# Recording the second layer's attention mixer and ordering it as one list-scheduled stage

## The chip, the cores and the metric

The kernel runs on one core of a Trainium2 chip. The metric is the device time of one execution in microseconds (us); the median of the runs is compared. PE is the matrix engine TensorE, PEld its weight loads, DVE is VectorE, ACT is ScalarE, POOL is GpSimd, SP is SyncE, which here mostly issues DMAs.

## The reference

The reference is a two-layer trunk on 16 learned tokens followed by 1024 inputs (1040 positions), width 1024. Layer 0 has an RWKV and pooling mixer, layer 1 a differential attention mixer; each is followed by an MLP. The attention, which is what matters here:

```python
def causal_diff_attention(q, k, v, lam):
    ...
        s = jnp.einsum('bqhcd,bkhcd->bhcqk', qblk, k).astype(jnp.float32) * scale
        qpos = start + jnp.arange(Q_BLOCK)
        mask = kpos[None, :] <= qpos[:, None]
        s = jnp.where(mask, s, -jnp.inf)
        p = jax.nn.softmax(s, axis=-1)
        attn = p[:, :, 0] - lam * p[:, :, 1]
        return jnp.einsum('bhqk,bkhe->bqhe', attn.astype(v.dtype), v)
    ...

def diff_attn_mixer(h, w_in, lam_vecs, subln_w, w_out, cos, sin, layer):
    ...
    q = apply_rope(q.reshape(B, L, DIFF_HEADS, 2, DIFF_HEAD), cos, sin)
    k = apply_rope(k.reshape(B, L, DIFF_HEADS, 2, DIFF_HEAD), cos, sin)
    ...
    o = causal_diff_attention(q, k, v, lam)
    o = rmsnorm(o, subln_w, SUBLN_EPS) * (1.0 - lam_init)
    return o.reshape(B, L, D_MODEL).astype(h.dtype) @ w_out
```

There are 8 heads; each has two halves c = 0, 1 of q and k, each half with a softmax of its own.

## The kernel before

Every fp32 product is made of three products of high and low parts, so matmuls come in triples (lines 377, 378 and 379 for the projections, 1895 to 1897 for the mix). `mixer1` is the attention mixer. `attn_in(h)` makes the input of head h: for k, q and v in turn, three chunks of 346 or so positions, each a group of 24 matmuls into one bank of the pool `dps` (two banks; `psq`, `psv`), then on DVE the rotary products `rp`, `ab` (`rows`), for k and q the DMAs that regroup the two halves into `qkd` (`heads`, eight issues on SP's queue for each of k and q), the casts to a high part on ACT and a low part on DVE (`halves`: `kh`, `kl`, `qst`); for v the product with `rsa` (`vt`), transposes `pst` and the casts `vh`, `vl` (`turn`). `rsa` holds 1/rms of each position; `settle` (line 485) sums squares over partitions with one matmul for a chunk of positions and makes it. The projections themselves read the unnormalized `opa` and do not need `rsa`; what follows them does.

`attn(h)` makes four groups g = 0 to 3 of two blocks of 128 queries. For each block `attn_block` makes scores `s` (two halves in the pool `sps`, two tiles), maximum, exp on ACT (line 1842), the sums and the difference `p` on DVE. `flip` transposes `p` to a single bank `tr` (`tps`), which ACT casts to `ah` and DVE to `al`; `tail` does it for the 16 last positions (`trx`, line 1879, one for each group); `mix` multiplies by v into the single bank `av`; `square` and `norm` finish a half of the head. `soft` in head h makes the blocks of the next group, or the first two blocks of head h+1. While `attn(h)` runs, the steps of `attn_in(h+1)` are written between its steps at the places of the table `at`; in the last head, steps of the output projection (`early`, tiles `pse`) are written there.

In `mixer1` all this is issued directly, and the framework decides each engine's order. The stage of layer 0 is made otherwise: a `Recorder` takes each instruction with a price for its engine and the regions it reads and writes; `Flow.order` then sorts them by a list schedule (the engine that can start earliest takes the ready task with the longest rest of chain) and `Flow.run` writes them out under `manual_schedule`, where this order holds. Ring buffers (`Ring`) fix which buffer each tile has. A task with no recorded writer before it counts as ready from the start.

Of the kernel before, what the change touches and what calls it, by code (L numbers as in the profile page):

```python
# [8 lines left out]
F32R = mybir.dt.float32r  # L9
# [190 lines left out]
class Recorder:  # L200
# [8 lines left out]
    @contextlib.contextmanager  # L209
    def group(self):  # L210

        self.held = []
        yield
        calls, self.held = self.held, None
        if calls:
            self.keep(calls[0][0], sum(c[1] for c in calls), [c[2] for c in calls], [x for c in calls for x in c[3]], [x for c in calls for x in c[4]], False, 0)
# [43 lines left out]
    def call(self, eng, op, args, kw):  # L260
# [12 lines left out]
        elif eng == "PE":  # L273
            cols, x = math.prod(int(k) for k in args[0].shape[1:]), args[1]
            if x.dtype == F32R:
# [46 lines left out]
class Trunk:  # L322
# [22 lines left out]
    def group(self):  # L345
        return self.nc.group() if isinstance(self.nc, Recorder) else contextlib.nullcontext()
# [1289 lines left out]
    def mixer1(self, hn):  # L1636
# [4 lines left out]
        with tc.tile_pool(name="dps", bufs=2, space=PSUM, reuse_waits="tile") as dps, \  # L1641
# [3 lines left out]
             tc.tile_pool(name="ep", bufs=1, reuse_waits="tile") as ep:  # L1645
            self.dps, self.sps, self.tps, self.aps, self.ep = dps, sps, tps, aps, ep
# [34 lines left out]
            for h in range(8):  # L1681
                nxt, side = self.attn_in(h + 1, hn) if h < 7 else (None, fill[:30])
                main = self.attn(h, qkv, nxt)
                at = (0, 6, 12, 12, 14, 15, 16, 24, 24, 24, 24, 24, 24, 24, 29, 29) if h < 7 else [0 + i * 2 for i in range(len(side))]
# [13 lines left out]
            self.late_x = xs  # L1698
        return part
# [101 lines left out]
    def attn_block(self, h, i, qkv):  # L1801
# [7 lines left out]
        for c in (0, 1):  # L1809
# [7 lines left out]
            for a in range(0, L, 512):  # L1817
# [8 lines left out]
                if x1 > x0:  # L1826
                    nc.tensor.matmul(out(x0, x1), self.identb, self.maskb[:, x0 - m0:x1 - m0], start=False, stop=True)
# [30 lines left out]
    def attn(self, h, qkv, nxt):  # L1858
# [27 lines left out]
        def mix(g, j0):  # L1886
# [5 lines left out]
            if j0 < 2 * g + 2:  # L1892
                for j in (j0, j0 + 1):
                    sl = slice((j - j0) * 256, (j - j0) * 256 + 256)
                    nc.tensor.matmul(o, vh[:, j], ah[:, sl], start=(j == 0), stop=False)  # L1895
                    nc.tensor.matmul(o, vl[:, j], ah[:, sl], start=False, stop=False)
                    nc.tensor.matmul(o, vh[:, j], al[:, sl], start=False, stop=False)
            else:
                o1, j = o[:, P:], j0
                nc.tensor.matmul(o1, vh[:NM, j], ah[:NM], start=False, stop=False)  # L1900
                nc.tensor.matmul(o1, vl[:NM, j], ah[:NM], start=False, stop=False)
                nc.tensor.matmul(o1, vh[:NM, j], al[:NM], start=False, stop=True)
# [35 lines left out]
        for g in range(4):  # L1938
# [145 lines left out]
```

## Time and profile before

| | |
|---|---|
| median of 3 runs | 2788.69 us (2782.02 to 2795.86) |
| the profiled execution's own time | 2794.32 us |
| span of its profile | 2792.5 us |
| mean granted clock of TensorE | 0.969 of full |
| PE busy | 2626.3 us, 94% of the span |
| DVE, ACT, POOL busy | 2043.4, 1345.2, 292.5 us |

The span is from the first instruction to the last. The attention mixer's part begins around 1406 us with its first projections and ends at 2039 us, where the output projection's last matmul of the stage starts. A busy PE is not PE at its peak, since matmuls overlap and their ends are modelled.

### The profile page before, as it was taken

The page shows a single profiled execution, that of the slowest core. Times are in us where ns is not written, and L with a number is a line of the kernel's source. Part 1 is how long each engine was busy: PE and PEld are TensorE (multiplying, and loading weights), DVE is VectorE, ACT ScalarE, POOL GpSimd, SP SyncE. Part 2 cuts the span into 40 slices and gives each one's busy share as a digit, 9 for nine tenths or more (in the row PEclk, how much of TensorE's full clock was granted, in tenths as well). Part 3 has the DMA queues.
Part 4 walks back from the last instruction along what each step waited for, and adds up shares of the span by engine and source line. Part 5 has one row for each costly group of instructions (what it writes and reads, how often), then busy time and mean ns, then how long its engine had stood idle before and what let it go on. Part 6 is the DMA issues. An engine that isn't in the chain of part 4 may idle for free.

```text
span 2792.5 us, 44856 instructions
## 1 busy us (share of the span) xinstructions
PE 2626.3 (94%) x16950; PEld 2389.0 (86%) x16950; DVE 2043.4 (73%) x3742; ACT 1345.2 (48%) x2779; POOL 292.5 (10%) x410
## 2 busy tenths in 40 slices
PE   7999997899999999999968999999889999999997
PEld 6899897799899999999957899898786788778877
DVE  5356866634977778888785887888648778778888
ACT  6456766544533335333334556556645333443342
POOL 0111334230000000000012222222000000000000
PEclk9999999899999999999978999999999999999998
DMA  4456767554423345443332222222243243553443
GB/s 154 168 191 193 233 207 220 175 148 156 146 107 148 146 172 191 168 153 135 99 113 69 61 74 71 61 67 63 81 153 130 106 166 131 197 185 136 151 159 121
DMA packets 198576, 391.28 MB, mean 140 GB/s; under 512 B 59984, under 2 KB 122328, under 8 KB 185944
## 3 DMA queue, kind: packets, MB, share of 16 engines
q1 hardware_dynamic: 171176, 348.24, 37.6%
q10 hardware_dynamic: 27184, 40.18, 4.0%
q8 instruction: 133, 2.18, 0.3%
q14 instruction: 83, 0.68, 0.1%
HBM read 240.06 MB, written 131.38 MB: 133 GB/s over the span
## 4 chain that ended last, share of the span: by engine, by line
PE 66%; DVE 9%; ACT 3%; issue 2%; DMA 2%; POOL 0%; SPq 0%; DVEq 0%; ACTq 0%; POOLq 0%
PE bank L690 46%; PE psq L377 2%; PE psq L378 2%; PE psq L379 2%; PE ps L292 1%; PE s L1823 1%; PE s L1825 1%; PE tr L1869 1%; PE xs L292 1%; ACT p L1842 1%; PE bank L732 1%; PE av L1895 1%; DVE ac L767 1%; DVE p L1855 1%; DVE ac L1072 1%
## 5 line engine op out<-in xcount | busy, mean ns | idle before, releaser
L690 PE MATMUL bank<-opa,wp 128*128 128x260 f32 (+1 forms) x3296 | 656.3, 319 | 5.8 <-DVE wp L781 3.5
L690 PEld LDWEIGHTS bank<-opa,wp 128*128 128x128 f32 x3296 | 517.2, 189 | 55.6 <-DVE wp L781 5.0
L690 PE MATMUL bank<-opb,wp 128*128 128x260 f32 (+1 forms) x1150 | 347.6, 323 | 3.0 <-DVE ac L1000 3.0
L292 PE MATMUL ps<-opa,whi 128*128 128x346 f32 (+2 forms) x1008 | 270.3, 330 | 5.3 <-DVE ys L292 4.1
L690 PE MATMUL bank<-opa,hh 128*128 128x260 f32 (+1 forms) x1112 | 240.8, 321 | 7.5 <-DVE hh L781 5.3
L690 PEld LDWEIGHTS bank<-opb,wp 128*128 128x128 f32 x1150 | 216.2, 188 | 22.1 <-ACT opa L1023 3.4
L1000 DVE TENSOR_TENSOR ac<-bank,ac 128x520 f32<-128x520 f32 (+1 forms) x256 | 171.1, 691 | 67.1 <-PE bank L690 65.1
L690 PE MATMUL bank<-opa,opb 128*128 128x260 f32 (+4 forms) x1168 | 204.7, 305 | 11.4 <-DVE opb L670 5.4
L690 PEld LDWEIGHTS bank<-opa,hh 128*128 128x128 f32 x1112 | 185.7, 191 | 24.0 <-DVE hh L781 5.8
L292 PEld LDWEIGHTS ps<-opa,whi 128*128 128x128 f32 x1008 | 182.2, 194 | 7.5 <-DVE ys L292 4.9
L690 PEld LDWEIGHTS bank<-opa,opb 128*128 128x128 f32 x1168 | 167.6, 193 | 22.3 <-DVE opb L670 5.8
L690 PE MATMUL bank<-opb,hh 128*128 128x260 f32 (+1 forms) x616 | 180.4, 326 | 0.0
L780 ACT CAST wp<-raw 128x512 fp32r<-128x512 f32 (+1 forms) x138 | 80.4, 584 | 199.3 <-PE bank L690 191.7
L292 PE MATMUL ps<-opa,wlo 128*128 128x346 f32 (+2 forms) x504 | 158.8, 315 | 0.0
L780 ACT CAST wp<-ss 128x512 fp32r<-128x512 f32 (+1 forms) x130 | 76.4, 589 | 165.4 <-PE bank L690 141.0
L1842 ACT ACTIVATE p<-s,m 128x272 f32<-128x272 f32 (+7 forms) x128 | 95.6, 751 | 86.1 <-DVE m L1838 84.4
L690 PE MATMUL bank<-opa,tt 128*128 128x260 f32 (+1 forms) x648 | 131.1, 320 | 2.2 <-DVE ac L1000 2.0
L690 PEld LDWEIGHTS bank<-opb,hh 128*128 128x128 f32 x616 | 117.5, 191 | 10.0
L377 PE MATMUL psq<-opa,wp 128*128 128x346 f32 (+2 forms) x352 | 118.0, 335 | 4.4 <-DVE rp L462 2.6
L362 POOL TENSOR_TENSOR wpx<-raw,wp 128x1024 fp32r<-128x1024 f32 (+1 forms) x14 | 34.4, 2459 | 789.6 <-PE bank L690 745.3
L379 PE MATMUL psq<-opa,wp 128*128 128x346 f32 (+2 forms) x352 | 113.9, 324 | 0.0
L690 PE MATMUL bank<-opb,opb 128*128 128x256 f32 (+4 forms) x456 | 111.3, 307 | 1.4 <-DVE tt L746 1.4
(408 smaller groups left out, 6587.4 us busy)
## 6 DMA issues: line engine op xcount, KB each, us to landing
raw<-in_w_dram SPq DMA_DIRECT2D x64, 1024.0 KB
hid<-ac SPq DMA_DIRECT2D x14, 1820.0 KB
hid<-ac SPq DMA_DIRECT2D x14, 1792.0 KB
hh<-hid SPq DMA_DIRECT2D x23, 1040.0 KB
hh<-hid SPq DMA_DIRECT2D x23, 1024.0 KB
pk<-sg ACTq DMA_DIRECT2D x32, 704.0 KB
lt<-pk SPq DMA_DIRECT2D x32, 704.0 KB
raw<-in_w_qkv_dram SPq DMA_DIRECT2D x24, 512.0 KB
```

The lines of the kernel that those rows point to most:

```text
L292: one = eng, cost, lambda: fn(*args, **kw), r, w
L362: (lo or nc.gpsimd).tensor_tensor(lw[:, :n], raw[:, :n], hi[:, :n].bitcast(F32), op=ALU.subtract)
L377: nc.tensor.matmul(ps, wh, xh, start=(first and i == 0), stop=False)
L378: nc.tensor.matmul(ps, wl, xh, start=False, stop=False)
L379: nc.tensor.matmul(ps, wh, xl, start=False, stop=(last and i == n - 1))
L690: nc.tensor.matmul(ps, use(x), use(y), start=start and i == j == 0, stop=i == len(ws) - 1 and j == 2, skip_group_check=not start)
L732: nc.tensor.matmul(acc, ones, use(src), start=first, stop=last)
L767: F.dve(NH, lambda mk=mk, k=k: stt(mk, mk, self.gcol(l, 1, k), y, op0=ALU.mult, op1=ALU.mult), r=nm + [("T", 2)], w=nm)
L780: F.act(n, lambda: nc.scalar.copy(use(t[0][:, :n]), src), r=rd, w=[z[0]] + claim)
L1000: F.dve(NH, lambda d=d, q=q: tt(sv(d), q, sv(d), op=ALU.add), r=nq + nd, w=nd, ps=True)
L1072: F.dve(W, lambda d=d, k=k: tt(d, d, use(H3[k // 4][:, k % 4, :W]), op=ALU.add), r=nd + [("H", k // 4, k % 4)], w=nd)
L1842: nc.scalar.activation(p[:, :L0], S[c][:, :L0], AF.Exp, bias=m2[:, c:c + 1], scale=0.125, accum_out=m2[:, 2 + c:3 + c])
```

## The change

`mixer1` makes a `Recorder`, wraps its pools in rings of the same sizes, and runs the flow at its end. The three matmuls of a score or of a mix step are kept together as one recorded task (`group`; with `whole` the task counts as writing its whole bank, for the first of a group of mixes). A transpose is priced at 0.115 in the recorder. The places of the next head's steps (`at`) and their sequence are changed, and `pair` takes the mix of two steps ago ahead of the flip. The computation and the number of instructions on the matrix of each head stay.

```diff
@@ class Recorder
-    def group(self):
+    def group(self, whole=False):
...
-            self.keep(calls[0][0], sum(c[1] for c in calls), [c[2] for c in calls], [x for c in calls for x in c[3]], [x for c in calls for x in c[4]], False, 0)
+            w = [x for c in calls for x in c[4]]
+            self.keep(calls[0][0], sum(c[1] for c in calls), [c[2] for c in calls], [x for c in calls for x in c[3]], [x.tensor[:] for x in w[:1]] if whole else w, False, 0)
...
-            if x.dtype == F32R:
+            if op == "transpose":
+                cost = .115
+            elif x.dtype == F32R:
...
@@ mixer1
+            rec = Recorder(tc)
+            self.nc = nc = rec
+            dps, sps, tps, aps = [Ring(x, n, least) for x, n, least in ((dps, 2, 512), (sps, 2, 1024), (tps, 1, 512), (aps, 1, 512))]
+            ep = Ring(ep, 1)
...
-                at = (0, 6, 12, 12, 14, 15, 16, 24, 24, 24, 24, 24, 24, 24, 29, 29) if h < 7 else [0 + i * 2 for i in range(len(side))]
+                if h < 7:
+                    side = [side[i] for i in (0, 1, 2, 3, 5, 6, 7, 10, 11, 4, 8, 9, 12, 13, 14, 15)]
+                at = (0, 6, 12, 12, 15, 16, 18, 20, 22, 25, 25, 25, 25, 25, 29, 29) if h < 7 else [0 + i * 2 for i in range(len(side))]
...
+            rec.flow.run()
+        self.nc = tc.nc
...
@@ attn_block
-                nc.tensor.matmul(out(a, b), st[:, qs], kh[:, a:b], start=True, stop=False)
                 x0, x1 = max(a, m0), min(b, L)
-                nc.tensor.matmul(out(a, b), st[:, qs], kl[:, a:b], start=False, stop=x1 <= x0)
...
+                with self.group():
+                    nc.tensor.matmul(out(a, b), st[:, qs], kh[:, a:b], start=True, stop=False)
+                    nc.tensor.matmul(out(a, b), st[:, qs], kl[:, a:b], start=False, stop=x1 <= x0)
...
@@ attn, mix
-                    nc.tensor.matmul(o, vh[:, j], ah[:, sl], start=(j == 0), stop=False)
...
+                    with self.group(j == 0):
+                        nc.tensor.matmul(o, vh[:, j], ah[:, sl], start=(j == 0), stop=False)
...
@@ attn, the order of flips and mixes
+                if i >= 2:
+                    pair.append(ms[i - 2])
                 if i < n:
                     pair.append(ts[i])
-                if i >= 2:
-                    pair.append(ms[i - 2])
```

In the changed program all instructions of the mixer have the recorder's line 295, and the tiles have the names of the rings: `ps_0` and `ps_1` are the two banks of `dps`, `s_0` and `s_1` those of `sps`, `vt_0` to `vt_2` a ring of three that `p` uses too, `spare` the ring of `vh` and `vl`. Outside the mixer the order of every engine is the same in both programs.

First place, PE where the stage begins. Before, 49 projection matmuls into `s` stand between the last matmul of the stage ahead (line 732) and the first `settle` (line 485); here are the last of them:

```order
L379 MATMUL s_13735<-opa_74,wp_6332 128x346
L377 MATMUL s_13735<-opa_75,wp_6332 128x346
L378 MATMUL s_13735<-opa_75,wp_6333 128x346
L379 MATMUL s_13735<-opa_75,wp_6332 128x346
L485 MATMUL ps_13848<-rsa,con 128x346
L378 MATMUL s_13737<-opa_70,wpx 128x332
L379 MATMUL s_13737<-opa_70,wp_6334 128x332
```

In the changed program the settle follows that last matmul at once:

```order
L735 MATMUL bank_6368<-ss_6356,con 128x346
L295 MATMUL ps_0_13735<-rsa,con 128x346
L295 MATMUL s_0_13728<-opa_70,wp_6332 128x348
L295 MATMUL s_0_13728<-opa_70,wp_6333 128x348
L295 MATMUL s_0_13728<-opa_70,wp_6332 128x348 x2
```

So the settle has moved ahead of those 49 projections.

Second place, DVE while head 0's input is finished: `kl` is the low part of k's halves, `rp` and `ab` here are the rotary products of head 1. Before:

```order
L1787 TENSOR_TENSOR vl_13875<-pst_14074,vh_13874 16x128
L1763 TENSOR_TENSOR kl_14009<-qkd_13998,kh_14008 128x640
L1731 TENSOR_TENSOR rp_14144<-psq_14119,cs 64x348
L1732 TENSOR_TENSOR rp_14144<-psq_14119,cs 64x348
L1731 TENSOR_TENSOR rp_14244<-psq_14219,cs 64x346
L1733 TENSOR_TENSOR ab_14118<-psq_14119,cs 128x348
L1732 TENSOR_TENSOR rp_14244<-psq_14219,cs 64x346
L1763 TENSOR_TENSOR kl_14014<-qkd_14003,kh_14013 128x640
```

Changed:

```order
L295 TENSOR_TENSOR vt_0_13741<-ps_0_13735,rsa 128x346
L295 TENSOR_TENSOR kl_0_13748<-qkd_0_13744,kh_0_13746 128x640
L295 TENSOR_TENSOR kl_1_13749<-qkd_1_13745,kh_1_13747 128x640
L295 TENSOR_TENSOR spare_1_13740<-ps_0_13735,spare_1_13738 128x512
L295 TENSOR_TENSOR spare_1_13740<-ps_1_13736,spare_1_13738 128x512
L295 TENSOR_TENSOR spare_1_13740<-ps_1_13736,spare_1_13738 16x128
L295 TENSOR_TENSOR rp_2_13734<-ps_0_13735,cs 64x348 x2
L295 TENSOR_TENSOR qst_0_13750<-qkd_0_13744,qst_0_13750 64x1024
```

Both halves of `kl` now stand together, ahead of head 1's rotary products; before, five of those stood between them.

Third place, PE in the last head, at the transposes of group 2 and the scores around them; `pse` before, and `ps_0` and `ps_1` after, are output projection work that fills. Before:

```order
L1827 MATMUL s_19690<-maskb,identb 128x128
L379 MATMUL pse_19543<-opa_73,wp_6332 128x256
L1869 MATMUL tr_19594<-con,p_19498 128x128
L1869 MATMUL tr_19594<-con,p_19473 128x128
L1869 MATMUL tr_19594<-con,p_19498 128x128
L1823 MATMUL s_19744<-kh_18790,qst_19023 128x512
L1825 MATMUL s_19744<-kl_18791,qst_19023 128x512
L1823 MATMUL s_19744<-kh_18790,qst_19023 128x512
L1895 MATMUL av_19707<-ah_19599,vh_19033 128x256
```

Changed:

```order
L295 MATMUL tr_0_13757<-con,vt_1_13742 128x128
L295 MATMUL tr_0_13757<-con,vt_2_13743 128x128
L295 MATMUL ps_0_13735<-opa_77,wp_6332 128x256
L295 MATMUL ps_0_13735<-opa_77,wp_6333 128x256
L295 MATMUL ps_0_13735<-opa_77,wp_6332 128x256
L295 MATMUL ps_1_13736<-opa_71,wp_6334 128x256
L295 MATMUL ps_1_13736<-opa_71,wpx 128x256
L295 MATMUL ps_1_13736<-opa_71,wp_6334 128x256
L295 MATMUL ps_0_13735<-opa_77,wp_6332 128x256
L295 MATMUL ps_0_13735<-opa_77,wp_6333 128x256
L295 MATMUL ps_0_13735<-opa_77,wp_6332 128x256
L295 MATMUL av_0_13764<-ah_2_13760,spare_0_13737 128x256
```

Where a transpose was followed by the next block's scores and the mix, three triples of filling work now stand between the transposes and the mix.

## Rows read from the trace of the kernel before

**Rows 1.** The page: busy time by engine, and the shares of the chain that ended last.

```profile
PE 2626.3 (94%) x16950; PEld 2389.0 (86%) x16950; DVE 2043.4 (73%) x3742; ACT 1345.2 (48%) x2779; POOL 292.5 (10%) x410
PE 66%; DVE 9%; ACT 3%; issue 2%; DMA 2%; POOL 0%; SPq 0%; DVEq 0%; ACTq 0%; POOLq 0%
```

**Rows 2.** Windows of the mixer: from:to and length in us, busy us (x instructions) of each engine, granted clock of PE, DMA share, GB/s.

```profile
1436.00:1490.00 54.00, 48.73 (x274) 46.45 (x275) 32.10 (x60) 13.28 (x23) 19.16 (x15) 0.92 0.24 60
1490.00:1555.00 65.00, 54.73 (x304) 45.57 (x303) 44.77 (x81) 34.08 (x69) 14.51 (x13) 0.87 0.26 71
1685.00:1750.00 65.00, 64.24 (x425) 58.41 (x424) 53.03 (x100) 38.02 (x76) 17.56 (x16) 1.00 0.24 66
1945.00:1985.00 40.00, 30.67 (x167) 23.39 (x166) 31.25 (x71) 27.52 (x68) 0.58 (x3) 0.90 0.21 67
1985.00:2025.00 40.00, 40.00 (x313) 38.10 (x312) 18.18 (x34) 21.54 (x50) 5.66 (x3) 0.97 0.25 81
```

**Rows 3.** Timeline of PE where the stage begins: start, duration, engine, line, out<-in, and in brackets the idle time before with what ended it.

```profile
1406.33 1.52 PE L732 MATMUL bank<-ss,con 128*128 128x346 f32 x2 [4.46 <-DVE ss L682]
...
1409.62 0.49 PE L377 MATMUL s<-opa,wp 128*128 128x348 f32 x1
1409.90 0.49 PE L378 MATMUL s<-opa,wp 128*128 128x348 f32 x1
...
1421.17 0.32 PE L379 MATMUL s<-opa,wp 128*128 128x346 f32 x1
1436.08 1.52 PE L485 MATMUL ps<-rsa,con 128*128 128x346 f32 x2 [14.60 <-DVE rsa L682]
```

**Rows 4.** Timeline of DVE while head 0's input is finished.

```profile
1474.46 0.83 DVE L1763 TENSOR_TENSOR kl<-qkd,kh 128x640 fp32r<-128x640 f32 x1 [0.61 <-ACT kh L1761]
...
1481.75 0.52 DVE L1731 TENSOR_TENSOR rp<-psq,cs 64x346 f32<-64x346 f32 x1 [2.86 <-PE psq L379]
...
1483.40 1.18 DVE L1763 TENSOR_TENSOR kl<-qkd,kh 128x640 fp32r<-128x640 f32 x1
...
1496.28 1.22 DVE L1756 TENSOR_TENSOR qst<-qkd,qst 64x1024 fp32r<-64x1024 f32 x1
```

**Rows 5.** Timeline of ACT there.

```profile
1480.43 1.05 ACT L1755 CAST qst<-qkd 128x1024 fp32r<-128x1024 f32 x1 [5.04 <-DMA qkd<-ab]
1489.74 1.05 ACT L1755 CAST qst<-qkd 128x1024 fp32r<-128x1024 f32 x1 [8.26 <-DMA qkd<-ab]
1499.39 0.38 ACT L1842 ACTIVATE p<-s,m 128x144 f32<-128x144 f32 x1 [8.60 <-DVE m L1838]
```

**Rows 6.** Timeline of PE: the transpose `trx` of group 3 in heads 0, 1, 2 and 6, and the last matmul of the stage.

```profile
1559.16 0.27 PE L1879 MATMUL trx<-con,p 128*16 128x128 f32 x1
...
1626.94 0.27 PE L1879 MATMUL trx<-con,p 128*16 128x128 f32 x1
...
1691.72 0.27 PE L1879 MATMUL trx<-con,p 128*16 128x128 f32 x1
...
1950.46 0.28 PE L1879 MATMUL trx<-con,p 128*16 128x128 f32 x1
...
2038.97 0.27 PE L379 MATMUL pse<-opa,wp 128*128 128x256 f32 x1
```

**Rows 7.** Timeline of PE: starts that follow each other without a wait, for projections of 346 columns (21 instructions lie between the two shown starts), a mix of 256, and scores of 512.

```profile
1467.09 0.33 PE L377 MATMUL psv<-opa,spare 128*128 128x346 f32 x1
...
1470.41 0.32 PE L377 MATMUL psv<-opa,spare 128*128 128x346 f32 x1
...
1745.00 0.28 PE L1896 MATMUL av<-ah,vl 128*128 128x256 f32 x1
1745.12 0.28 PE L1897 MATMUL av<-al,vh 128*128 128x256 f32 x1
...
1525.58 0.39 PE L1825 MATMUL s<-kl,qst 128*128 128x512 f32 x1
1525.81 0.34 PE L1823 MATMUL s<-kh,qst 128*128 128x400 f32 x1
```

**Rows 8.** PE in one steady head by tile, in this order: `psq`, `psv`, `av`, `tr`, `s`. Window, length, busy us (x instructions), clock, DMA share, GB/s.

```profile
1685.00:1750.00 65.00, 25.89 (x144) 1.00 0.24 66
1685.00:1750.00 65.00, 11.84 (x72) 1.00 0.24 66
1685.00:1750.00 65.00, 12.46 (x73) 1.00 0.24 66
1685.00:1750.00 65.00, 6.79 (x43) 1.00 0.24 66
1685.00:1750.00 65.00, 13.96 (x70) 1.00 0.24 66
```

**Rows 9.** Waits by engine, line and what was waited for: us in total, times, longest us. The first two in 1945 to 1990 us, the last in 1685 to 1750 us.

```profile
PE tr L1869 <- DVE p L1855: 4.0, 3, 2.2
PE s L1823 <- ACT p L1842: 2.8, 3, 1.8
...
DVE qst L1756 <- ACT qst L1755: 0.3, 1, 0.3
```

**Rows 10.** Timeline of SP's queue in head 0: the eight DMA issues of q's regrouping; the duration is from the first issue to the last one's end.

```profile
1607.46 5.26 SPq L1747 DMA_DIRECT2D qkd<-ab  x8
```

More of the change, by code (lines that the diff above doesn't have):

```diff
@@ L343, in nm, with group @@
         return f"{s}{self.uid}"
-    def group(self):
-        return self.nc.group() if isinstance(self.nc, Recorder) else contextlib.nullcontext()
+    def group(self, whole=False):
+        return self.nc.group(whole) if isinstance(self.nc, Recorder) else contextlib.nullcontext()
     def weights(self, src, n=1024, lo=None, pool=None):
@@ L1822, in attn_block @@
                     out = lambda x0, x1: se[:, c * NM + x0 - 1024:c * NM + x1 - 1024]
-                nc.tensor.matmul(out(a, b), st[:, qs], kh[:, a:b], start=True, stop=False)
                 x0, x1 = max(a, m0), min(b, L)
-                nc.tensor.matmul(out(a, b), st[:, qs], kl[:, a:b], start=False, stop=x1 <= x0)
-                if x1 > x0:
-                    nc.tensor.matmul(out(x0, x1), self.identb, self.maskb[:, x0 - m0:x1 - m0], start=False, stop=True)
+                with self.group():
+                    nc.tensor.matmul(out(a, b), st[:, qs], kh[:, a:b], start=True, stop=False)
+                    nc.tensor.matmul(out(a, b), st[:, qs], kl[:, a:b], start=False, stop=x1 <= x0)
+                    if x1 > x0:
+                        nc.tensor.matmul(out(x0, x1), self.identb, self.maskb[:, x0 - m0:x1 - m0], start=False, stop=True)
             S.append(sp)
@@ L1894, in mix @@
                     sl = slice((j - j0) * 256, (j - j0) * 256 + 256)
-                    nc.tensor.matmul(o, vh[:, j], ah[:, sl], start=(j == 0), stop=False)
-                    nc.tensor.matmul(o, vl[:, j], ah[:, sl], start=False, stop=False)
-                    nc.tensor.matmul(o, vh[:, j], al[:, sl], start=False, stop=False)
+                    with self.group(j == 0):
+                        nc.tensor.matmul(o, vh[:, j], ah[:, sl], start=(j == 0), stop=False)
+                        nc.tensor.matmul(o, vl[:, j], ah[:, sl], start=False, stop=False)
+                        nc.tensor.matmul(o, vh[:, j], al[:, sl], start=False, stop=False)
             else:
                 o1, j = o[:, P:], j0
-                nc.tensor.matmul(o1, vh[:NM, j], ah[:NM], start=False, stop=False)
-                nc.tensor.matmul(o1, vl[:NM, j], ah[:NM], start=False, stop=False)
-                nc.tensor.matmul(o1, vh[:NM, j], al[:NM], start=False, stop=True)
+                with self.group():
+                    nc.tensor.matmul(o1, vh[:NM, j], ah[:NM], start=False, stop=False)
+                    nc.tensor.matmul(o1, vl[:NM, j], ah[:NM], start=False, stop=False)
+                    nc.tensor.matmul(o1, vh[:NM, j], al[:NM], start=False, stop=True)
         sb = lambda: ep.tile([P, 512], F32, tag="sb", name=self.nm("sb"), bufs=4)
```

## The prediction

> **What bounds the kernel now.** I read the page first, then windows over the mixer, then single timelines. PE is busy 94% of the span and makes 66% of the chain that ended last, with DVE at 9% [rows 1]; the change touches nothing outside the mixer, so the rest of the program's time is taken as it is. Inside the mixer the windows show three different places [rows 2]. A steady head (1685 to 1750) has PE busy 64.24 of 65 us at full clock: nothing else is the limit there. The opening (1436 to 1555) has only 274 + 304 = 578 matmuls in 119 us where a steady head has 425 in 65: PE idles 5.27 + 10.27 = 15.5 us, and the clock, at 0.92 and 0.87, costs another 0.08 x 54 + 0.13 x 65 = 12.8 us. The tail (1945 to 1985) has PE busy 30.67 of 40 us, 9.3 idle, with a clock of 0.90, and the 40 us behind it 0.97: 4.0 + 1.2 = 5.2 us more. So what an order can give back is some 28 us in the opening, 14.5 in the tail, and little in a steady head.
>
> The stage splits at markers, the transpose of group 3's last 16 positions [rows 6]: the opening and head 0 end at 1559.16; six heads follow to 1950.46 (391.3 us; 67.8 for the first, 64.8 each for the others); the tail ends with the last matmul at 2038.97 (88.5 us).
>
> **The change part by part.** No instruction is added or removed, so each price is one of waits and of places. What a matmul costs PE without a wait is the distance of starts [rows 7]: 0.158 us for a projection ((1470.41 - 1467.09) / 21), 0.12 for a mix, 0.23 for 512 score columns.
>
> *Opening and head 0.* What it loses: before, the first 49 projections run from 1407.7 to 1421.2, at 0.28 us each, in time in which PE otherwise waits for the row sums; it then idles 14.60 us until the settle at 1436.08 [rows 3]. In the changed order the settle stands first, and PE takes its queue in order, so these 49 run after 1436: 49 x 0.158 = 7.7 us (13.7 if all went at half the clock). No other engine covers that.
>
> What it gives: before, DVE makes the first `kl` at 1474.46, then stands behind head 1's rotary products, which wait for projections (2.86 us at 1481.75), and reaches the second `kl` only at 1483.40 [rows 4]. q's second regrouping waits on it, ACT's casts of q wait 5.04 and 8.26 us for it, the low part of q ends on DVE at 1497.5, and the first exp starts at 1499.39 [rows 5]. By then PE has done five chunks of head 1's projections, which it lacks afterwards, when head 0's softmax leaves it idle. In the new order the two `kl` stand together. Following the new rows by hand with the durations of these views, I get 1456 for the settle of the third chunk, 1466 for k's DMAs, both `kl` at 1474 to 1476, the q DMAs from 1480, and the first exp near 1490, nine us earlier in spite of the 7.7.
>
> How much of it reaches the end: from the settle to the end of head 0 the new order has 687 matmuls: 462 projections at 0.158 = 73.0; 57 mixes at 0.12 = 6.8; 61 transposes and the like at 0.11 = 6.7; 22,080 score columns at 0.23 per 512 = 9.9; masks, tails, settles and norm, an estimate, 6. That is 102 us. Before, without the 49, it was 102 - 7.7 = 94.3, against 1559.16 - 1436.08 = 123.1 in the trace: 28.8 lost, which agrees with the 28.3 of the windows. After, I keep 11 of it: the half clock at the start, which no edit touches (some 4), and 7 of waits for the settles, the first DMAs and the single `tr` bank. So it ends at 1436.1 + 102 + 11 = 1549, **-10 us**. The bounds: if nothing is won but the 49 are late, +8; if only the clock's 3 are left, -18.
>
> *Six heads.* One head is 216 projections [rows 8] x 0.158 = 34.1; 60 mixes x 0.12 + 12 tails x 0.16 = 9.1; 56 transposes x 0.11 = 6.1; scores of 18,944 columns = 8.5 and 20 masks that hold up the next matmul by about 0.12 = 2.5; norm and the 16 column scores 2.2: 62.5 us, against 64.8. The Trainium skill ("Perfetto Trace Analysis", section "Identifying the Most-Contended Engine") says that matmul busy time misleads, since matmuls are pipelined, and that the busy share of the weight loads tells more. Here that share is 58.41 of 65 [rows 2], which by that rule would leave 6.6 us a head or 39 in six; the busy row alone would leave 0.76, or 4.6 in six; the trace's distances stand between them at 2.3.
>
> At most 2.3 x 6 + 3 (the first interval's excess) = 16 us are there. I take 0.5 for each of five heads and 2.5 of the 3, since the new places spread the input of head 1: **-5 us**. A fixed order that fits worse than the old one costs; I bound it by 1 us a head, the size of the idle that a steady head has now (0.76): +6.
>
> *Tail.* Before, transposes wait 4.0 us for `p` and scores 2.8 for ACT's exps [rows 9], while projection triples that could run stand behind them in PE's queue; in the new order such triples stand between transposes, scores and mixes. Of 9.3 idle and 5.2 clock I take 7 and 4: **-11 us**. The bounds: 0, if the waits only move, and -14, if all is filled. Behind the last norm as many filling matmuls are left as before, so the end has no new gap.
>
> *Edits at nothing.* The transposes' price, the groups of three, the table `at` and the sequence in `pair` only move places in the list, and are in the three terms. Groups cost nothing while PE has other work; without it a group waits for its latest input, within the bound of 1 us a head.
>
> **The sum.** -10 - 5 - 11 = -26. The profiled execution took 2794.3 (span 2792.5) and would take 2768 (span 2766.5); it lies 5.6 above the median of the runs, so the median goes from 2788.7 to **2763**. All bounds on one side: -48 (2741) and +14 (2803).
>
> **The rivals.** *Only the opening moves.* In a steady head PE is busy 64.24 of 65, and the tail's waits are those of a chain (scores, exp, `p`, transpose) that no order shortens. For it: DVE and ACT are busy 31.25 and 27.52 of the tail's 40 us [rows 2]. Against it: the filling triples need nothing of that chain. Time 2779 (-8 to -18).
>
> *Nothing comes back.* The 7.7 us of deferred projections are paid and the earlier exp only moves where PE waits next, at the softmax of head 0: 2789 to 2797.
>
> *Slower: q's DMAs come too late in every head.* The recorder prices an issue on SP at 0.47; the row has 5.26 / 8 = 0.66 for each of eight [rows 10], so k and q together are 3 us later than the list believes. DVE's order, now fixed, has `qst` ahead of the `al` of group 3's flips, so the single `tr` bank stays full, and PE with its transposes stands. At 3 us a head and seven heads it takes back 21 of the 26; it makes the kernel slower by more than 14 us from (26 + 14) / 7 = 5.7 a head. With the 8.26 that ACT waits at this place in the opening [rows 5] it is 26 - 58 = 32 slower: 2821. Against it: `qst` waits 0.3 us in a steady head now [rows 9], and in both orders it stands among the same `al`.
>
> **How the numbers follow.** About 14 us (0.5%) is what the runs, 2782 to 2796, can tell from no change. Chances: the forecast 0.60 (all faster); only the opening 0.15 (0.07 faster, 0.08 same); nothing back 0.13 (same); slower 0.12. So faster 0.67, same 0.21, slower 0.12. The range reaches from 2740, all gains, to 2803, all losses within the bounds; it leaves out the slower rival and a little below. The forecast's own range is 2745 to 2774.
>
> **What would show it.** The settle at 1436 with the 49 projections behind it; the first exp near 1490; the `tr` transpose of 16 positions of head 0's group 3 near 1549, of head 6 near 1935, the last matmul near 2013; a clock above 0.95 in the tail. I am wrong if the first exp stays near 1499, if the steady heads take over 65 us, or if `qst` waits for `qkd` over 2 us in a steady head.

## The result and the profile after

The changed kernel takes 2798.61 us (median of 12 runs, 2789.99 to 2806.78), the kernel before 2789.18 us in 12 runs beside it (2780.71 to 2797.76): ratio 1.0035, 95% interval 1.0023 to 1.0047. That is 9.4 us slower, a small loss within the 0.5% that the prediction called no change, but with so many runs its sign is clear; 2763 was forecast. The profiled execution took 2806.78 us (span 2805.0), 8 above its median, as that of before was 5 above its own. Of run e3 below, the profiled execution was a slow one (span 2878.2 us), so only the order of its rows is used.

Page of the changed kernel, busy time by engine and the chain that ended last:

```profile
PE 2617.9 (93%) x16950; PEld 2383.0 (85%) x16950; DVE 2034.1 (73%) x3742; ACT 1346.3 (48%) x2779; POOL 292.1 (10%) x410
PE 63%; DVE 10%; ACT 4%; DMA 2%; issue 2%; POOL 0%; SPq 0%; DVEq 0%; ACTq 0%; POOLq 0%
```

PE is less busy in a longer span, and DVE and ACT have taken 2 points of the chain from it [rows 1]: the instructions are as many as before, the waits are more. Windows of the changed kernel's mixer (columns as in [rows 2]):

```profile
1437.00:1490.00 53.00, 48.88 (x276) 47.02 (x277) 29.51 (x53) 14.79 (x24) 16.22 (x13) 0.91 0.26 71
1490.00:1555.00 65.00, 59.75 (x386) 52.14 (x384) 50.08 (x95) 35.41 (x75) 18.44 (x14) 1.00 0.24 66
1685.00:1750.00 65.00, 63.22 (x414) 57.02 (x413) 49.62 (x99) 37.84 (x76) 16.38 (x14) 1.00 0.23 65
1945.00:1985.00 40.00, 28.27 (x161) 22.87 (x160) 30.75 (x66) 26.41 (x63) 3.24 (x4) 0.79 0.25 68
```

Beside [rows 2], the second part of the opening has 82 matmuls more and the full clock; the steady head has 11 fewer in the same 65 us; the tail has 6 fewer, and its clock is 0.79 instead of 0.90. PE of the changed kernel, where the stage begins, and four of its group-3 tails (heads 0, 5, 6, 7; the transpose is now named `tr`, as ring buffers share names):

```profile
1407.91 1.52 PE L735 MATMUL bank<-ss,con 128*128 128x346 f32 x2 [4.47 <-DVE ss L685]
1437.75 1.49 PE L295 MATMUL ps<-rsa,con 128*128 128x346 f32 x2 [28.32 <-DVE rsa L685]
...
1559.10 0.27 PE L295 MATMUL tr<-con,vt 128*16 128x128 f32 x1
...
1889.52 0.27 PE L295 MATMUL tr<-con,vt 128*16 128x128 f32 x1
...
1973.24 0.27 PE L295 MATMUL tr<-con,vt 128*16 128x128 f32 x1
...
2028.18 0.27 PE L295 MATMUL tr<-con,vt 128*16 128x128 f32 x1
```

To compare executions I count from the last matmul of the stage ahead, the second of the two in the first row (1407.1 before, 1408.6 after), and note these markers for every kernel. The end of a head is the start of its group-3 tail. The four steady heads are the intervals from the end of head 1 to the end of head 5. "Next stage" is the 31st matmul of the stage behind the mixer, the same instruction in every kernel; from there on its matmuls follow each other 0.12 us apart in all of them. The end is from the last `norm`'s matmul to it.

| us | settle | first exp | end head 0 | end head 1 | end head 5 | end head 6 | end head 7 | last norm | next stage |
|---|---|---|---|---|---|---|---|---|---|
| before | 29.0 | 92.3 | 152.1 | 219.9 | 479.1 | 543.4 | 610.5 | 618.1 | 645.7 |
| after | 29.1 | 86.8 | 150.5 | 216.3 | 480.9 | 564.6 | 619.5 | 624.0 | 654.2 |
| e1 | 29.0 | 91.8 | 155.1 | 227.4 | 519.2 | 593.0 | 664.4 | 670.3 | 696.8 |
| e2 | 29.1 | 86.8 | 149.0 | 216.7 | 490.3 | 577.6 | 631.2 | 635.6 | 667.0 |
| e4 | 29.1 | 87.5 | 151.2 | 216.0 | 478.6 | 543.2 | 613.2 | 617.6 | 648.3 |
| e5 | 42.6 | 85.6 | 149.0 | 214.0 | 478.3 | 559.4 | 615.8 | 620.3 | 651.4 |
| e9 | 29.0 | 79.1 | 142.4 | 207.3 | 472.0 | 552.8 | 607.8 | 612.2 | 642.5 |
| e12 | 35.3 | 76.5 | 137.4 | 203.6 | 466.1 | 530.3 | 600.1 | 604.5 | 635.1 |
| e13 | 29.1 | 83.8 | 144.1 | 209.5 | 470.7 | 558.3 | 613.2 | 617.0 | 649.2 |

Read across, after against before: the end of head 0 comes 1.6 us earlier (10 were forecast), head 1 gives 2.0 more, the four heads behind it lose 5.4 (1.35 each; 64.8 became 66.15), the stretch from head 5's tail to the last norm loses 4.1 (head 6 alone loses 19.4, and what follows it wins 15.3 back), the end 2.6. That is 8.5 us up to the next stage. Behind that marker, where the order is the same, the profiled execution takes 2.4 more; it lies 3 us further above its median than that of before does. So of the 9.4 some 1 has no place here.

**The opening.** ACT of the changed kernel, the second cast of q and the first exp:

```profile
1489.03 1.05 ACT L295 CAST qst<-qkd 128x1024 fp32r<-128x1024 f32 x1 [2.96 <-DMA qkd<-ab]
1495.41 0.38 ACT L295 ACTIVATE vt<-s,m 128x144 f32<-128x144 f32 x1 [5.33 <-DVE m L295]
```

The wait for q's DMAs fell from 8.26 [rows 5] to 2.96 and the exp comes 5.5 us earlier, counted from the zero. From exp to the end of head 0, though, it is 63.7 us, where it was 59.8. Windows from the settle to the end of head 0, of before and of the changed kernel (columns as in [rows 2]):

```profile
1436.00:1559.16 123.16, 107.62 (x605) 95.86 (x606) 78.90 (x144) 49.41 (x94) 33.67 (x27) 0.89 0.25 65
```

```profile
1437.75:1559.10 121.35, 112.73 (x690) 102.72 (x691) 82.85 (x155) 51.81 (x103) 35.73 (x29) 0.96 0.24 66
```

In nearly the same time PE does 85 matmuls more. Of projections there are 462 where before had 391: the 49 that now follow the settle, and 22 more of head 1's.

**The tail.** Waits of PE between 1947 and 1968 (timeline of the changed kernel), then PE's `ps` matmuls alone in four stretches of 10 us (busy us, count, clock, DMA share, GB/s):

```profile
1949.58 0.33 PE L295 MATMUL tr<-con,vt 128*128 128x128 f32 x1 [1.14 <-DVE m L295]
...
1954.49 0.47 PE L295 MATMUL tr<-con,vt 128*128 128x128 f32 x1 [3.40 <-ACT p L295]
...
1967.91 0.45 PE L295 MATMUL s<-kh,qst 128*128 128x400 f32 x1 [1.82 <-ACT p L295]
```

```profile
1930.00:1940.00 10.00, 6.03 (x35) 1.00 0.14 43
1940.00:1950.00 10.00, 1.17 (x7) 1.00 0.32 103
1950.00:1960.00 10.00, 2.35 (x12) 0.60 0.62 152
1960.00:1970.00 10.00, 0.00 (x0) 0.67 0.10 34
```

`ps` holds head 7's projections, a few transposes and norms, and then the output projection. The projections run densely until 1937; then PE has little but head 6's chain of scores, exp, `p` and transpose, whose end lies 21 us later than before (564.6 against 543.4). It idles, and the clock falls with it. Here are the tail of head 6's group 2 (counting from 0) and, for before, a stretch of `psv`, the last of head 7's projections; then the changed kernel's tail of group 2:

```profile
1924.05 0.27 PE L1879 MATMUL trx<-con,p 128*16 128x128 f32 x1
...
1930.00:1940.00 10.00, 9.25 (x59) 1.00 0.56 131
```

```profile
1945.84 0.27 PE L295 MATMUL tr<-con,vt 128*16 128x128 f32 x1
```

Counted from the end of head 5, group 2 was done after 37.9 us before, with 59 projections still to run behind it; in the changed kernel it is done after 56.3, when the projections are gone. Head 7 then takes only 54.9 us, as its input is long ready, but at its end 9.0 are lost against before, 7.2 of them since head 5.

**Steady heads.** Waits of PE over four heads (us in total, times, longest), of the changed kernel (1625 to 1890) and of before (1627 to 1886):

```profile
PE s L295 <- ACT vt L295: 2.6, 3, 0.9
PE tr L295 <- DVE vt L295: 1.4, 4, 0.4
PE tr L295 <- DVE ah L295: 1.4, 2, 1.1
PE ps L295 <- DVE ab L295: 1.1, 3, 0.4
PE ps L295 <- DVE spare L295: 0.5, 3, 0.2
```

```profile
PE pst L1784 <- DVE vl L1787: 2.9, 4, 0.8
```

7.0 us of named waits against 2.9: 1.0 of the 1.35 a head. The other suspect is interleaving. PE of the changed kernel where a triple of projections stands alone between scores:

```profile
1896.62 0.41 PE L295 MATMUL ps<-opa,wp 128*128 128x346 f32 x1
1896.86 0.32 PE L295 MATMUL ps<-opa,wpx 128*128 128x346 f32 x1
1897.02 0.32 PE L295 MATMUL ps<-opa,wp 128*128 128x346 f32 x1
```

From the first start to the second 0.24 us, to the third 0.16. Counted in the trace, a steady head has 28 such runs of projections, 16 before, and the first matmul of each costs about 0.09 (0.06 before) over 0.158: 2.5 us a head against 1.0. These 1.5 and the 1.0 of waits are together more than the 1.35 that is lost, so they don't simply add.

**The end.** PE's waits behind the last norm:

```profile
2035.55 0.39 PE L295 MATMUL ps<-opa,wp 128*128 128x256 f32 x1 [1.66 <-ACT pz L295]
...
2056.43 0.58 PE L693 MATMUL bank<-opa,opb 128*128 128x256 f32 x1 [7.07 <-ACT opb L672]
2057.85 2.50 PE L693 MATMUL bank<-opa,opb 128*128 128x256 f32 x10 [0.84 <-DVE opb L673]
```

In the trace of before these are 0.46, 2.53 and 4.54 us: nearly all of the wait for the next stage's operand now lies ahead of its first matmul, and the sum grows from 7.5 to 9.6. The rest of the 2.6 goes with 114 matmuls behind the last norm, where before has 108.

### The profile page after: what moved, and what is told of

Same layout as the page of the kernel before. It is cut to its first block, busy times and chain, and to the rows that moved or that the text cites. A ratio compares the mean times of both kernels' runs of the same rounds, so it can differ in the third digit from the quotient of the medians.

```text
span 2805.0 us, 44863 instructions
## 1 busy us (share of the span) xinstructions
PE 2617.9 (93%) x16950; PEld 2383.0 (85%) x16950; DVE 2034.1 (73%) x3742; ACT 1346.3 (48%) x2779; POOL 292.1 (10%) x410
## 4 chain that ended last, share of the span: by engine, by line
PE 63%; DVE 10%; ACT 4%; DMA 2%; issue 2%; POOL 0%; SPq 0%; DVEq 0%; ACTq 0%; POOLq 0%
PE bank L693 46%; PE ps L295 9%; PE s L295 3%; PE av L295 2%; ACT vt L295 1%; PE tr L295 1%; PE xs L295 1%; DVE m L295 1%; ACT p L295 1%; PE bank L735 1%; DVE vt L295 1%; DVE ac L770 1%; DVE ac L1075 1%; DVE opb L820 1%; DVE ac L1074 1%
## 5 line engine op out<-in xcount | busy, mean ns | idle before, releaser
L295 PE MATMUL ps<-opa,wp 128*128 128x346 f32 (+3 forms) x1600 | 346.0, 326 | 8.2 <-DVE spare L295 3.1
L295 PEld LDWEIGHTS ps<-opa,wp 128*128 128x128 f32 x1600 | 259.9, 190 | 20.3 <-issue 4.7
L783 ACT CAST wp<-ss 128x512 fp32r<-128x512 f32 (+1 forms) x130 | 76.5, 589 | 166.6 <-PE bank L693 143.7
L693 PEld LDWEIGHTS bank<-opa,tt 128*128 128x128 f32 x648 | 102.8, 190 | 11.8 <-ACT opb L1026 2.2
```

The source lines that it names most:

```text
L295: one = eng, cost, lambda: fn(*args, **kw), r, w
L693: nc.tensor.matmul(ps, use(x), use(y), start=start and i == j == 0, stop=i == len(ws) - 1 and j == 2, skip_group_check=not start)
L783: F.act(n, lambda: nc.scalar.copy(use(t[0][:, :n]), src), r=rd, w=[z[0]] + claim)
```

## The experiments

Theory at first: the recorder's list is right in kind, but knows two things wrongly. A task with no recorded writer is ready at once (so the settle, which really waits for `rsa`, goes first and 49 projections go behind it), and the longest rest of chain ranks all of head 7's input above head 6's attention. Rivals: the edits of places cost the time, not the recorder; the list's prices are wrong; or PE's finer interleaving is the cost itself. Ratios are to runs of the kernel before on the same chip.

**Places or recorder.** The kernel before with the new `at`, the new sequence of steps and the new `pair`, without the recorder (e1), and the changed kernel with the old ones (e2):

```diff
@@ e2, on the changed kernel
-                if h < 7:
-                    side = [side[i] for i in (0, 1, 2, 3, 5, 6, 7, 10, 11, 4, 8, 9, 12, 13, 14, 15)]
-                at = (0, 6, 12, 12, 15, 16, 18, 20, 22, 25, 25, 25, 25, 25, 29, 29) if h < 7 else ...
+                at = (0, 6, 12, 12, 14, 15, 16, 24, 24, 24, 24, 24, 24, 24, 29, 29) if h < 7 else ...
@@ and in pair, ms[i - 2] behind ts[i] again
```

> The kernel before with only the new table at, the new sequence of the next head's steps and the new sequence of flips and mixes; no recorder, no fixed order. If the loss comes from the recorder's list (the settle ahead of 49 projections, head 7's projections ahead of head 6's attention), this is the time of before within 5 us (2784 to 2794). If the new places themselves hurt, it is 5 to 15 us slower, and a steady head takes about 66 us here as well.

> The changed kernel with the old table at, the old sequence of the next head's steps and of flips and mixes, so the recorder, rings and groups alone. If the recorder's list is the cause, it is as slow as the changed kernel, within 5 us of 2798. If the new places are the cause, it is at or below the time of before, 2789.

e1: 2844.46 us (2840.18 to 2847.46), ratio 1.021 [1.0186, 1.0234]. e2: 2810.3 us (2804.02 to 2812.15), ratio 1.0085 [1.006, 1.0109]. In e2 the ring of `ah` and `al` holds two flips, so a mix written behind the flip two steps on reads that flip's values; its instructions are the same, but its waits are not quite those of a real kernel, and the number is a rough one. Without the recorder the new places make each head 73 us long. Waits of PE in e1, 1560 to 1925:

```profile
PE tr L1871 <- ACT p L1846: 8.5, 5, 1.7
PE tr L1871 <- DVE p L1857: 7.9, 9, 1.5
PE pst L1786 <- DVE vl L1789: 4.6, 5, 0.9
```

So neither half alone is better than the two together. With the new places the framework's order makes transposes wait for `p`, 16.4 us in five heads; which of the three edits of places does it, e1 does not tell. The transposes' price and the groups were taken out in no run.

**The opening.** Tasks that read `rsa` get a time before which the list doesn't take them; in e3 20 us on all engines, in e5 15.3 us and 17 for v's weights (`spare`), on PE alone, in e9 the `rsa` part on all engines again:

```diff
-        ready = [0.0] * len(T)
+        ready = [self.late.get(i, 0.0) for i in range(len(T))]
@@ Recorder.keep, e9 (e5: if eng == "PE" alone)
+        for name, m in r:
+            for part, t in self.hold:
+                if part in name and (eng == "PE" or part == "rsa"):
+                    self.flow.late[i] = max(self.flow.late.get(i, 0.0), t)
@@ mixer1 (e5: in layer 0's mixer too)
+            rec.hold = (('rsa', 15.3), ('spare', 17.0))
```

> The changed kernel, but the list is told that rsa is ready only 20 us into the stage, so that 110 projection matmuls stand ahead of the first settle. If the deferred projections were a loss that nothing covers, this gives back 110 x 0.158 = 17 us at most, and 8 or more: 2781 to 2790. If the opening is bound by the chain behind the settle and PE has slack there anyway, under 3 us. If one of the early projections waits for v's weights, the settle starts later than 1438 and it is slower than the changed kernel.

> The changed kernel, with the list told on PE that rsa is ready 15.3 us and v's weights 17 us into the stage: 91 projections of k and q stand ahead of the first settle and none of v's, so that the settle stands at its old time. If the deferred projections are a loss of 0.158 us each, the end of head 0, counted from the settle, falls from 121.4 to 107 to 114 us and the time by 7 to 14 us, to 2784 to 2791. If the stage behind the settle is bound by the chain to the first exp and not by PE, the end of head 0 moves by under 3 us and the time stays at 2795 to 2798.

> The changed kernel with the list told that rsa is ready 15.3 us into the stage for every engine, and v's weights 17 us for PE. In the run that told PE alone, two triples of q stood behind DVE's rp, which waited 16.37 us, and the settle slid from 29.1 to 42.6 us behind the matmul ahead of the stage. Here all 96 projections of k and q stand ahead of both, and the settle should be back at 29.1. If the deferred projections were the loss, the first exp comes 8 or more us earlier than 86.8 behind that matmul, and the time falls to 2783 to 2791. If v's weights, which POOL finishes 37 us behind that matmul, now stop PE instead, the first exp is at 84 to 87 and the time stays at 2795 to 2798.

e3: 2801.46 us, 1.0051 [1.0031, 1.0071]. e5: 2796.22 us, 1.0028 [1.0012, 1.0044]. e9: 2791.19 us (2784.69 to 2795.34), 1.0008 [0.9997, 1.002]. PE in e3, in e5 and in e9:

```profile
1505.01 0.66 PE L297 MATMUL ps<-opa,spare 128*128 128x348 f32 x1 [15.61 <-ACT spare L297]
```

```profile
1437.45 0.66 PE L297 MATMUL s<-opa,wp 128*128 128x346 f32 x1 [16.37 <-DVE rp L297]
...
1440.30 1.36 PE L297 MATMUL ps<-rsa,con 128*128 128x346 f32 x2
```

```profile
1427.30 1.52 PE L297 MATMUL ps<-rsa,con 128*128 128x346 f32 x2 [4.64 <-DVE rsa L691]
...
1540.73 0.27 PE L297 MATMUL tr<-con,vt 128*16 128x128 f32 x1
```

In e3 v's projections are taken ahead of the settle, and PE, in order, waits for v's weights: a second input that the list believed ready. In e5 the settle comes 13.5 us late behind a projection that waits 16.37 us for DVE's `rp` of the same bank. By those two alone, the deferred projections seemed worth nothing. In e9, which holds the `rsa` readers of DVE too, that wait is gone: PE waits 4.64 us ahead of the settle instead of 28.32, the end of head 0 comes 8.1 us earlier, and the ratio falls from 1.0035 to 1.0008, 7.5 us. So work ahead of the settle is worth having. The price of 7.7 for 49 projections is not shown by it, though: e9 moves 96 ahead, 15.2 us at 0.158, and some of that goes to waits for v's weights just behind the settle (2.89 and 1.87 us).

**The tail.** Head 6's attention steps get a rank of at least 80 us, so they no longer stand behind all of head 7's input (e4); with e5's hold as well (e7):

```diff
+            rank[i] = max(rank[i], self.floor.get(i, 0.0))
@@ mixer1, around each step f()
+                    a = len(rec.flow.tasks)
                     f()
+                    if h in (6,):
+                        rec.flow.floor.update((j, 80) for j in range(a, len(rec.flow.tasks)))
```

> The changed kernel, but the attention steps written in head 6 have at least a rank of 80 in the list, so that head 7's projections no longer pass them. If the early use of those projections leaves PE without work in 1945 to 1985, the transpose trx of head 6 comes 10 to 20 us earlier, the clock there stays above 0.9, and the time falls by 5 to 10 us to 2788 to 2794. If the tail is bound by head 7's softmax chain whatever stands beside it, under 3 us.

> The settle behind 91 projections and the rank of 80 for head 6's attention, together. If the opening and the tail are two separate losses, their gains add: some 10 us for the tail and 7 to 14 for the opening, so 2774 to 2781. If the opening's gain is swallowed by what waits later, it is where the rank alone is, 2785.

e4: 2784.83 us (2778.45 to 2791.8), 0.9998 [0.9981, 1.0014]. e7: 2791.65 us, 1.0009 [0.9992, 1.0026]. Head 6's tail is at 1942.23 in e4 and at 1973.24 in the changed kernel; here are windows from some 33 us before it to 7 behind it, of the changed kernel and of e4:

```profile
1940.00:1980.00 40.00, 29.02 (x158) 22.89 (x159) 30.14 (x66) 27.44 (x64) 3.78 (x6) 0.79 0.29 81
```

```profile
1910.00:1950.00 40.00, 36.59 (x244) 32.12 (x242) 34.54 (x67) 27.51 (x60) 9.63 (x9) 1.00 0.35 96
```

244 matmuls at full clock instead of 158 at 0.79. That one number changed in the list takes the ratio from 1.0035 to 0.9998, 10 us, so the ranks are shown as a cause. Of the 10 the table places 6: the stretch from head 5 to the last norm is 4.1 shorter, the heads ahead of it 2.3, for the rank reaches back to them too. The rest has no place in the one profiled execution. But e4's stretch from head 5 to the last norm is 139.0 us, as before's is: the tail is as it was, not 11 us better. e7's opening is like e5's (settle at 42.6, head 0 ends at 149.8), and it adds nothing to e4.

**The list's prices.** ACT out of PSUM and masks priced nearer to the trace (e6), that with e7's rank and, in the attention mixer alone, its hold (e8), and e6 with SP's issue at 0.63 instead of 0.47 (e10):

```diff
+            if self.fit and psum and not wide:
+                cost = n / 1200 + (.145 if kw.get("accum_out") is not None else .045)
-                cost = max(cols / 2400 + .01, .06)
+                cost = cols / 2400 + .07 if self.fit else max(cols / 2400 + .01, .06)
-            cost = {"POOL": 1.0, "SP": .47}.get(eng, .38)
+            cost = {"POOL": 1.0, "SP": .63 if self.slow else .47}.get(eng, .38)
```

> The changed kernel with three prices of the recorder set to what the trace of the changed kernel shows from start to start, in the attention mixer alone: ACT on PSUM at elements / 1200 + 0.045, an exp with its sum 0.1 more, a mask matmul at 0.125. If the 66.0 us of a steady head come from scores and transposes that the list puts too early, because exps of 1.09 us are priced 0.79, a steady head falls to 64.5 to 65.3 and the time by 4 to 8 us. If the longer heads come from how finely the triples are interleaved, a steady head stays at 66.0 within 0.3.

> The same with the three prices as well. If all three causes stand and add, 2768 to 2777 and a steady head of 64.5 to 65.3; if the prices are nothing, the same as without them.

> The kernel with the three measured prices, and an issue on SP's queue at 0.63 instead of 0.47, as the traces have it from start to start. With the three prices alone a steady head took 71 us, and scores waited for qst 1.8 us in each. If q's DMA issues, priced too low, are why, that wait goes below 0.5 us and a steady head falls to 64.5 to 67; if the list only happens to fall into a worse pattern, the head stays above 68 with another wait in its place.

e6: 2806.29 us, 1.0075 [1.0059, 1.0091]. e8: 2801.05 us, 1.0046 [1.0026, 1.0066]. e10: 2795.61 us, 1.0027 [1.0006, 1.0049]. Waits of PE in e6 over four heads (1545 to 1826):

```profile
PE s L298 <- DVE qst L298: 7.4, 4, 2.3
PE s L298 <- ACT p L298: 4.4, 4, 1.1
```

Truer prices made it worse: the list now believes q's input early, puts scores where `qst` is not there yet, and PE waits 1.85 us a head; most of its heads take 71 us. This is the slower rival's cause (issues on SP priced too low), met on PE. With 0.63 that wait is gone and the heads take 67. Prices decide, but nearer prices don't give shorter heads: e10's are no shorter than the changed kernel's 66, so these prices are not what makes those longer. e8 has e6's long heads again (up to 72.1 us).

**Handoffs.** The list's delays between engines times 1.5, with e4's rank (e11):

```diff
-        delay = lambda e, same: (AFTER[e][same] if self.fine else 0.0 if same else .3)
+        delay = lambda e, same: (AFTER[e][same] * self.room if self.fine else 0.0 if same else .3)
```

> The changed kernel with the rank of 80 for head 6's attention, and every delay of the list between engines times 1.5. If a steady head's 66.0 us come from chains that the list places too tightly, PE's waits in a steady head fall from 1.7 to under 1 us and the head to 64.5 to 65.5, the time to 2776 to 2782. If looser chains only take another place, the head stays at 66 and the time at 2785 within 5.

2782.03 us (2778.43 to 2787.51), 0.9979 [0.9965, 0.9992], with heads of 66.4. More distance does not shorten the steady heads, and the time is e4's within the intervals. It does shorten the opening: head 0 ends at 140.4, 111.3 us behind a settle that still stands ahead of every projection, where the changed kernel takes 121.35. Here is e11's window from the settle to the end of head 0:

```profile
1425.39:1536.70 111.31, 107.37 (x675) 98.92 (x676) 77.81 (x145) 49.83 (x94) 34.48 (x28) 0.98 0.27 72
```

PE idles 3.9 us instead of 8.6, at a clock of 0.98 instead of 0.96, and does 15 matmuls fewer. e10 and e13 keep the settle first as well and end head 0 at 144.0 and 144.1. So the deferred projections were not all of the opening's loss: how the list orders what follows the settle moves it by 6 to 10 us too.

**Interleaving.** Two (e13) or four (e14) projection triples as one task, nothing else changed:

```diff
+        for j in range(0, n, k):
+            with self.group():
+                for i, ((wh, wl), (xh, xl)) in three[j:j + k]:
```

> The changed kernel with two projection triples recorded as one task of six matmuls in the attention mixer, so that other work cuts in half as often. In the changed kernel a steady head has 28 runs of projections and the first matmul of each is 0.09 us longer than the next, before 16. If this is why a steady head takes 66.0 us and not 64.8, the runs fall to 20 or fewer and the head to 64.5 to 65.4. If the waits for exps and transposes are the reason, coarser tasks make them longer and the head takes 66 or more.

> The same with four triples as one task of twelve matmuls (1.9 us). If the number of runs decides, the head is at 64.5 or below; if a scheduler needs short fillers beside the transposes' 2 us cycle, waits for tr and s grow and the head takes 67 or more.

e13: 2789.26 us, 1.0009 [0.9994, 1.0023]. e14: 2796.12 us, 1.0034 [1.0016, 1.0051]. The wait of PE that costs most in e13, 1618 to 1878:

```profile
PE tr L296 <- DVE vt L296: 2.1, 4, 0.8
```

Counted in the steady heads of before, after, e13 and e14: runs of projections a head 16, 28, 22, 15; the extra of their first matmuls 1.0, 2.5, 1.2, 0.7 us; the mean length of heads 2 to 4 is 64.8, 66.4, 65.0, 65.6 us. e13 brings the heads nearly back, and the opening gains 6 us; its stretch from head 5 to the last norm is 3 us longer than after's. PE's listed waits in these three heads are 0.7, 2.15, 0.8 and 1.8 us a head, in the same order. e14 comes nearest to taking away the runs alone: its heads are 0.8 shorter than the changed kernel's, and what they still lose, 0.8, goes with its waits (it has other waits in other places, for a task of 12 matmuls moves the rest too). So both the runs and the waits go with the heads' length, and no run takes one away with nothing else changed: their shares stay open.

**Together.** Head 0's k and q chunks first, the settle held at 15.3 us, `spare` at 20, rank 80 for head 6 (e12); the same with two triples and rank 75 (e15):

```diff
-            for i in [0, 5, 1, 6, 10, 11, 2, 7, 3, 4, 12, 8, 9, 13, 14, 15]:
+            for i in [0, 5, 1, 6, 2, 7, 3, 4, 8, 9, 10, 11, 12, 13, 14, 15]:
```

> The rank of 80 for head 6, rsa ready at 15.3 us, v's weights at 20, and head 0's steps written with all of k and q ahead of v. If the opening is bound by the chain settle, k, kl, q, first exp, in which PE's in-order queue stands behind v's weights, the first exp comes 15 us or more earlier than 86.8 behind the matmul ahead of the stage and the end of head 0 at least 8 us earlier: 2770 to 2778. If head 0's softmax then only starves PE by as much, 2783 to 2788.

> k and q of head 0 ahead of v, the settle behind 96 projections, a rank of 75 for head 6's attention, and two triples as one task. If the runs of projections are the rest of the loss, five heads give another 5 us beside the 2775 of the version without them: 2768 to 2772. If not, 2774 or more.

e12: 2774.87 us (2765.92 to 2780.34), 0.9946 [0.9927, 0.9965]: it beats both kernels. e15: 2788.16 us, 1.0004 [0.9988, 1.002]. The opening in e12, PE's rows and a window:

```profile
1433.75 0.74 PE L298 MATMUL ps<-rsa,con 128*128 128x346 f32 x2
...
1535.82 0.27 PE L298 MATMUL tr<-con,vt 128*16 128x128 f32 x1
```

```profile
1490.00:1555.00 65.00, 63.19 (x417) 57.14 (x416) 49.78 (x99) 38.90 (x77) 16.13 (x16) 1.00 0.25 70
```

By the table, e12 ends head 0 14.7 us ahead of before and head 1 16.3 ahead; it gives back 3.3 in the next four heads, wins 0.6 to the last norm and loses 3.0 in the end. So a better opening and e4's tail stand in one kernel side by side; whether they add to the microsecond is not shown, since e12's opening was not run alone. The larger task of e15 doesn't add to them (its tail, head 6 to head 7, is 75.2 us, e12's 69.8).

## Why the prediction was wrong, step by step

By the prediction's own markers the forecast missed in two of its three terms: opening -10 forecast and -1.6 measured, six heads -5 and +22.8, tail -11 and -12.7. Together that is +8.5 at the stage's last matmul, counted from the zero, where -26 was forecast; the row is the changed kernel's, to be set beside the last of [rows 6].

```profile
2049.08 0.28 PE L295 MATMUL ps<-opa,wp 128*128 128x256 f32 x1
```

**Opening, -10 forecast, -1.6 measured.** The settle came at its place, with the 49 projections behind it, and both `kl` stood together, as read [rows 3, 4]; the exp came 5.5 us earlier and not 9. Mis-sized was what PE still loses behind the settle: I kept 11 us over 102 of work, and it was 121.35 - 102 = 19.4. By the window shown above, idle time is 8.6 and the clock costs 0.04 x 121 = 4.9, together 13.5, not far from 11. The other 6 are in a busy PE, whose matmuls take longer there than the prices of [rows 7]. That is no fault of the new order, for before has it too. I took before's work as the new one's without the 49 projections, 94.3 us, but its window has 605 matmuls and not 638: 71 projections fewer, and some scores and masks. That makes it some 89 us (an estimate, by the same prices). Its loss is then 34 us, of which idle time and clock are 15.5 + 13.5 = 29, and 5 are left in a busy PE as well. So the check that seemed to bear out the prices, 28.8 against 28.3, agreed by luck: too much work hid prices that were too low. The 11 was not out of reach in itself. e11, with its settle in the same place and nearly the same work, loses some 11 behind it.

**Six heads, -5 forecast, +22.8 measured.** This is the step that failed most: the bound of 1 us a head. The first head gave 2.0 (2.5 forecast); then the four lost 1.35 each instead of gaining 0.5, and head 6 took 83.7 us instead of 64.3. I took the bound from the idle time of a steady head. That measures the old order, and says nothing of how badly a new one fits, or of a head whose filling work the list has given away. The Trainium skill's rule ("Perfetto Trace Analysis", "Identifying the Most-Contended Engine"), by which weight loads tell the distance that is left, would have 8.0 us a head in the changed kernel (an estimate from 57.02 of 65); in no run do heads 2 to 4 take less than 64.8 in the mean, so none shows the gain that this rule leaves.

**Tail, -11 forecast, -12.7 measured, and not won.** "Such triples stand between transposes, scores and mixes" holds in head 7, which I read from the order, and head 7 is 12 us shorter. But the sum counted this as a gain for nothing. Filling needs work that is still there when the waits come: in head 6, one step earlier, the list had spent it, and from head 5's end to the last norm 4.1 us are lost. I bounded the term's loss at 0, as if a wait could only move; the clock of 0.79, where I said above 0.95, shows what was left out: with less to do, PE here also ran slower. In e4 the work is back in head 6, and head 7 takes 70.0 us and the stretch before's 139.0. The shortest of any run is 137.2 (e8), so none shows a gain of 11 there; for the tail the runs side with the rival "only the opening moves". "The end has no new gap" was wrong by 2.6 us, and 114 matmuls are left behind the last norm, not as many as before.

**Edits at nothing.** That they only move places was no reason for calling them free: with the framework's order they cost 2.1% (e1), with the recorder their absence costs about 0.5% (e2, roughly). What the transposes' price and the groups are worth stays open.

**The rivals.** "Nothing comes back" (2789 to 2797) is nearest, and nearly right on the opening; it had no loss in heads and tail. The slower one named q's DMAs. Over four steady heads of the changed kernel (1625 to 1890), `qst` on DVE waits for ACT, 1.5 us at most, and ACT 1.2 us once for the DMA; PE waits for `qst` nowhere, so it was not that. It did appear in e6.

```profile
ACT qst L295 <- DMA qkd<-ab: 1.2, 1, 1.2
DVE qst L295 <- ACT qst L295: 2.8, 6, 1.5
```

## What to carry to other kernels

A list schedule that ranks by the rest of the chain spends the next iteration's work early, and has none left to cover the last iteration's waits: look for the filler at the end of the loop, one iteration ahead of the gap. Give the list a ready time for each input that another stage makes, on every engine that reads it, or an engine in order stands behind the first that is late. Before you trust prices, count in the old trace the instructions that they are checked on; a count taken from the diff can be wrong by as much as the prices are. Judge a new order by markers at the end of each iteration, where a gain that is given back later is seen at once, and at instructions that are the same in both.

## What the runs showed of the hardware

The first projection behind another kind of matmul takes 0.24 us to the next start where the ones behind it take 0.16 (rows above); in the mean over steady heads it takes 0.09 more in the changed kernel and 0.06 more before. The granted clock followed what PE was given to do: in the stretch 1490 to 1555 it went from 0.87 [rows 2] to 1.00 with 82 matmuls more, which is 8 us, and in 1950 to 1960 it fell to 0.60, near the lower level (1.2 of 2.4 GHz), behind waits of 1 to 3 us each.
